# New durations and a price for a change of tile shape in the planner that orders a recurrence's instructions

## The chip, the cores and the metric

One core of one Trainium2 chip. The metric is the device time of one execution in microseconds (us); lower is better. Engines: PE is TensorE, DVE is VectorE, ACT is ScalarE, POOL is GpSimd, SP issues most of the DMAs.

## What is computed

One layer of a diffusion backbone over 1024 latent tokens with a prefix of 256 context tokens, width 1024:

```
h = modulate(rmsnorm(x))
u, rw, gates = split(h @ w_in)
a = s5_branch(u)                     # bidirectional complex SSM, then GELU and GLU (two dense products)
b = rwkv7_branch(rw)                 # 16 heads of 64, two directions, the recurrence below, then w_out
x = x + gate * ((sigmoid(ga) * a + sigmoid(gb) * b) @ w_out)
x = x + gate * conv_ffn(modulate(rmsnorm(x)))
out = rmsnorm(x)

# the recurrence, for each head and direction, over 256 + 1024 tokens
S = S * diag(w_t) + (S a_t) b_t^T + v_t k_t^T
y_t = S r_t
```

The token recurrence is computed in chunks of 64 tokens (20 chunks: 4 of context, 16 of latents). Within a chunk it becomes small matrix products, the inverse of a triangular 64x64 matrix for each head, direction and chunk, and a state that passes from chunk to chunk.

## The kernel before, in words

Three stages follow one another. Stage A computes the input projection, the S5 branch and the operands of the recurrence, and stores them to DRAM. Stage B (`stage_b`, line 1519 on) runs the recurrence, and as filler two large dense products. Stage C computes the output projections and the feed-forward part. The change touches stage B alone.

Stage B loops over 8 pairs of heads (`pair`); a pair holds both directions. Its work is written as nodes of a graph (`Node`, line 721), each with an engine, a cost in us, its dependencies and a function that emits its instructions:

- `prep_nodes` (line 905): for a block of 4 chunks and one direction. It loads kk, k and r (line 936), forms the gate projection `zn` on PE (L947, two 64-row products side by side), takes tanh of it twice (L955), a scan (L961), two exponentials (L962, L964), several products on DVE (L966 to L979) and one on POOL (L970), then the score products `sc` (L994, L997) and transposes `tp` (L1022, L1025) on PE in 64x64 tiles, which ACT and DVE copy out (L1002 copies the triangular matrix L).
- `inverse_nodes` (line 1041): for a batch of 8, 8 or 4 chunks (`BATCHES`). It sends L through DRAM into lanes (L1065, L1067), solves 16x16 blocks with 15 products (L1073) and 15 reductions (L1076) on DVE that follow one another, returns the result through DRAM (L1080 to L1088), and joins the blocks by five groups of products in 32x32 tiles (`merge`, L1109, L1115, L1120, L1137, L1142), whose last copies write TX (L1149). One set of lanes and one set of merge tiles serve all batches.
- `chain_nodes` (line 1157): for each chunk the state step. `gx` on PE, X copied by ACT (L1227), `gu` on PE with TX, U copied by DVE (L1244), `gs` on PE, the new state by DVE (L1267); `y` on PE and its copy on ACT (L1287). All its products are in 64x64 tiles (L1184, L1189).
- `final_nodes` (line 1313): for each pair four pieces of 256 tokens. They load y, the bonus, v and the gate from DRAM (L1326), normalise (products at L1330 and L176, small DVE steps at L155 to L163) and store.
- `filler_nodes` (line 1421): two dense products, 512 nodes of three full 128x128 matmuls with 512 columns (L1464, L1465, L1466). One node follows the other; their weights are split into two parts by ACT and DVE (L1443, L1444).

A ring of 5 blocks (`NBLK`) holds the prepared operands. One pair has 5 blocks, so a block's preparation for the next pair begins when the chain has read the same block of this pair and stored its output.

`Plan.order` (line 748) decides the order. It computes a due time for each node, back from the chain's steps through the costs and a lag per engine (`LAG`), stretched by 2. Then it simulates the engines: whichever node is ready and has the earliest due time goes next on its engine, and the engine's clock advances by the node's cost. The list in which nodes were taken is the order in which their instructions are emitted, and PE, ACT and DVE run their instructions strictly in that order (`manual_schedule`, line 1616). On PE the planner keeps a sum of columns (`n.cols`) over the last 3.4 us of its own time:

```python
if total < FORCE or cold and ticks.get(tick, 0.0) < HOT:
    best = pick(fills)
best = best or pick(h)
if best is None and (total < WARM or not left):
    best = pick(fills)
```

So a filler (or a product of a final) goes ahead of the recurrence when the sum is under `FORCE` (3600), and into an empty place when it is under `WARM` (4500). `pick(h)` takes the node with the earliest due time whose PSUM bank is free. The costs are numbers in the code; they are not read from a run, and the planner's time is not the chip's.

Of the kernel before, what the change touches and what calls it, by code (L numbers as in the profile page):

```python
# [720 lines left out]
class Node:  # L721

    __slots__ = ("eng", "cost", "deps", "succ", "emit", "due", "take", "give", "left", "ready", "bank", "cols", "fill", "tag", "key", "pri", "second")

    def __init__(self, eng, cost, deps, emit):
        self.eng, self.cost, self.emit = eng, cost, emit
        self.deps = [x for x in deps if x is not None]
        self.succ, self.due, self.take, self.give, self.ready = [], 1e9, None, None, 0.0
        self.cols, self.fill, self.tag, self.key, self.second = 0.0, None, None, False, None
# [7 lines left out]
class Plan:  # L737
# [19 lines left out]
    def order(self):  # L757
# [43 lines left out]
        def pick(h):  # L801

            skip, best = [], None
# [14 lines left out]
        while True:  # L818
# [8 lines left out]
            for e in heaps:  # L827
# [9 lines left out]
                if h or (e == "p" and fills):  # L837
# [6 lines left out]
                    else:  # L844
# [4 lines left out]
                        best = best or pick(h)  # L849
# [12 lines left out]
            n = best  # L862
            if n.eng == "p":
                hot.append((now, n.cols))
# [8 lines left out]
            end = now + n.cost  # L873
# [30 lines left out]
def prep_nodes(E, g, c0, d, k):  # L904
# [37 lines left out]
    zn.cols = 2048  # L942
# [7 lines left out]
    for half in range(2):  # L950
# [6 lines left out]
        th.append(op("a", 0.36, [zn, ms], tanh, give=zs[half]))  # L957
    ts_ = op("v", 0.2, [th[0]], lambda: nc.vector.tensor_scalar(P[:, :, 1:65], P[:, :, 1:65], 0.5, 0.5, op0=OP.mult,
                                                                op1=OP.add))
    flat = P.rearrange("p c t -> p (c t)")  # L960
    scan = op("v", 0.34, [ts_], lambda: nc.vector.tensor_tensor_scan(flat, E.m65, flat, 0.0, op0=OP.mult, op1=OP.add))  # L961
    epi = op("a", 0.4, [scan], lambda: nc.scalar.activation(PI, P[:, :, 1:65], AF.Exp, scale=KAP,  # L962
                                                             bias=E.ln_half))
    ep = op("a", 0.31, [epi], lambda: nc.scalar.activation(P, P, AF.Exp, scale=-KAP))  # L964
    pc = op("g", 0.1, [ep], lambda: nc.gpsimd.tensor_copy(g.PC.tile[:, d, c0:c0 + nb], P[:, :, 64]))
    q = [op("v", 0.4, [ep, lkk], lambda: nc.vector.scalar_tensor_tensor(  # L966
        Q[:, :, 0:64], v3(o_(kk)), -1.0, P[:, :, 0:64], op0=OP.mult, op1=OP.mult))]
    t1 = op("v", 0.34, [th[1]] + q, lambda: nc.vector.scalar_tensor_tensor(kk, o_(ta), 1.0, kk, op0=OP.add,
                                                                           op1=OP.mult))
    tid = op("g", 0.54, [t1], lambda: nc.gpsimd.tensor_scalar(ta, ta, E.par("ka", j), E.ka2[:, j:j + 1], op0=OP.mult,  # L970
                                                              op1=OP.add))
    tk = op("v", 0.34, [tid, lkx], lambda: nc.vector.tensor_mul(ta, ta, o_(kx)))
    bk = [op("v", 0.4, [t1, epi], lambda: nc.vector.tensor_mul(BK[:, :, 0:64], v3(o_(kk)), PI))]
# [936 lines left out]
```

## Time and profile before

| | us |
|---|---|
| median of 3 runs | 3253.95 |
| lowest, highest run | 3245.26, 3255.84 |
| the profiled execution | 3263.26 |
| its span, first to last instruction | 3261.5 |
| busy in the span: PE, DVE, ACT, POOL | 2911.9, 1838.5, 1371.0, 471.7 |

The rows below come from the one profiled execution. Times in them are us from the start of its span. A row of instruction groups gives the line of the kernel, the engine and operation, output and inputs, the count, then busy us and the mean ns of one, then the idle time of the engine just before them with what ended it. The ends of matmuls are modelled, so the spacing of their starts is the safer reading. "PEld" is the weight load of a matmul. "Clock" is the granted clock of PE as a share of 2.4 GHz: 1.0 is 2.4 GHz, 0.5 is 1.2 GHz. Some matmul records are missing from the trace. A product in float32 has two matmul records.

### The profile page before, as it was taken

How to read it: one execution, taken by the hardware profiler on the slowest of the kernel's cores; microseconds unless marked ns; L12 is line 12 of the kernel's file. 1: busy time of each engine (PE TensorE's matmuls, PEld its weight loads, DVE VectorE, ACT ScalarE, POOL GpSimd, SP SyncE). 2: the span in 40 equal slices, each digit the busy share in tenths (PEclk: the TensorE clock that was granted, in tenths of full speed). 3: DMA queues.
4: the chain of work that ended last, by engine and by line, in shares of the span. 5: the costliest groups of instructions: out<-in, count | busy, mean ns of one | idle time of the engine just before them, and what ended most of it. 6: DMA issues, size and time to landing. Idle time of an engine off the chain costs nothing.

```text
span 3261.5 us, 83856 instructions
## 1 busy us (share of the span) xinstructions
PE 2911.9 (89%) x34806; PEld 2197.0 (67%) x34806; DVE 1838.5 (56%) x4640; ACT 1371.0 (42%) x3055; POOL 471.7 (14%) x781
## 2 busy tenths in 40 slices
PE   6999887878579898999889888899998999999998
PEld 1788676767446666666666666666775888887876
DVE  7668777663345454668575667655534444344343
ACT  5224544435235454555444555442314433333332
POOL 0430011011222222223131222211000000000000
PEclk8999898989789888889788998889998999999999
DMA  5663333333465565455555455544531111113332
GB/s 190 207 168 104 128 117 125 110 119 120 145 167 148 152 161 135 120 135 133 130 143 126 119 141 146 125 125 139 193 120 55 52 48 49 46 52 112 107 107 74
DMA packets 556879, 399.32 MB, mean 122 GB/s; under 512 B 374225, under 2 KB 460497, under 8 KB 555217
## 3 DMA queue, kind: packets, MB, share of 16 engines
q1 hardware_dynamic: 517824, 300.96, 33.5%
q0 software_dynamic: 29312, 87.75, 8.0%
q10 hardware_dynamic: 9360, 5.25, 0.8%
q8 instruction: 273, 4.47, 0.6%
q14 instruction: 110, 0.89, 0.1%
HBM read 286.16 MB, written 112.85 MB: 122 GB/s over the span
## 4 chain that ended last, share of the span: by engine, by line
PE 61%; DMA 11%; issue 9%; DVE 9%; ACT 5%; SPq 3%; POOL 1%; ACTq 0%; DVEq 0%; POOLq 0%
PE pd L202 8%; PE pd L203 8%; PE pd L204 8%; PE bank L1464 5%; PE bank L1465 3%; PE bank L1466 3%; PE bank L1189 3%; PE bank L1184 3%; PE o L1751 3%; PE o L1752 3%; PE o L1753 2%; DMA wraw<-win 2%; PE bank L1330 1%; PE bank L994 1%; PE bank L947 1%
## 5 line engine op out<-in xcount | busy, mean ns | idle before, releaser
L189 DVE TENSOR_TENSOR wlo<-wraw,whi 128x512 fp32r<-128x512 f32 x276 | 184.0, 689 | 493.6 <-ACT whi L188 492.9
L188 ACT ACTIVATE whi<-wraw 128x512 fp32r<-128x512 f32 x276 | 165.8, 627 | 490.8 <-PE pd L203 243.4
L202 PE MATMUL pd<-hh,whi 128*128 128x512 f32 (+1 forms) x744 | 285.8, 384 | 51.8 <-ACT xs L624 35.2
L1464 PE MATMUL bank<-fxh,fwh 128*128 128x512 f32 x512 | 277.4, 542 | 12.1 <-ACT fo L1487 8.6
L202 PE MATMUL pd<-h2h,whi 128*128 128x512 f32 x704 | 275.5, 392 | 12.3 <-ACT h2h L1639 12.2
L204 PE MATMUL pd<-hh,wlo 128*128 128x512 f32 (+1 forms) x744 | 280.9, 378 | 1.5 <-DVE wlo L189 1.5
L203 PE MATMUL pd<-hl,whi 128*128 128x512 f32 (+1 forms) x744 | 282.1, 379 | 0.0
L204 PE MATMUL pd<-h2h,wlo 128*128 128x512 f32 x704 | 278.9, 397 | 0.0
L203 PE MATMUL pd<-h2l,whi 128*128 128x512 f32 x704 | 278.3, 396 | 0.3 <-DVE h2l L1640 0.2
L1465 PE MATMUL bank<-fxl,fwh 128*128 128x512 f32 x512 | 221.2, 432 | 0.5 <-issue 0.5
L1466 PE MATMUL bank<-fxh,fwl 128*128 128x512 f32 x512 | 220.8, 431 | 0.0
L202 PEld LDWEIGHTS pd<-hh,whi 128*128 128x128 f32 x744 | 148.3, 199 | 81.6 <-ACT xs L624 38.3
L204 PEld LDWEIGHTS pd<-hh,wlo 128*128 128x128 f32 x744 | 147.7, 199 | 25.8 <-DVE wlo L189 2.0
L203 PEld LDWEIGHTS pd<-hl,whi 128*128 128x128 f32 x744 | 148.4, 199 | 23.8 <-issue 2.5
L202 PEld LDWEIGHTS pd<-h2h,whi 128*128 128x128 f32 x704 | 133.2, 189 | 45.7 <-ACT h2h L1639 15.6
L203 PEld LDWEIGHTS pd<-h2l,whi 128*128 128x128 f32 x704 | 133.2, 189 | 33.0 <-DVE h2l L1640 2.1
L204 PEld LDWEIGHTS pd<-h2h,wlo 128*128 128x128 f32 x704 | 133.6, 190 | 26.6
L1464 PEld LDWEIGHTS bank<-fxh,fwh 128*128 128x128 f32 x512 | 104.3, 204 | 62.0 <-issue 20.0
L1444 DVE SCALAR_TENSOR_TENSOR fwl<-fr,fwh 128x512 fp32r<-128x512 f32 x128 | 92.6, 724 | 86.9 <-ACT fwh L1443 86.3
L1073 DVE TENSOR_TENSOR PR<-TN,LN 128x1 f32<-128x1 f32 (+9 forms) x360 | 118.5, 329 | 39.8 <-DMA LN<-LD 35.6
L1751 PE MATMUL o<-ph,whi 128*128 128x512 f32 x352 | 137.8, 396 | 2.2 <-ACT p L1725 2.2
L1752 PE MATMUL o<-pl,whi 128*128 128x512 f32 x352 | 138.9, 395 | 0.0
(395 smaller groups left out, 7209.3 us busy)
## 6 DMA issues: line engine op xcount, KB each, us to landing
wraw<-up SPq DMA_DIRECT2D x88, 256.0 KB
wraw<-down SPq DMA_DIRECT2D x88, 256.0 KB
wraw<-win SPq DMA_DIRECT2D x68, 256.0 KB
fin<-wmod SPq DMA_DIRECT2D x32, 512.0 KB
fr<-win SPq DMA_DIRECT2D x64, 256.0 KB
fr<-glu SPq DMA_DIRECT2D x64, 256.0 KB
s5U<-u_d SPq DMA_DIRECT2D x32, 320.0 KB
kk<-kk_d SPq DMA_DIRECT2D x80, 128.0 KB
```

The source lines that it names most:

```text
L188: nc.scalar.activation(hi[:, c], raw, AF.Copy)
L189: nc.vector.tensor_sub(lo[:, c], raw, hi[:, c])
L202: nc.tensor.matmul(pt[:, :n], hi[:, c], xh, start=k == 0, stop=False)
L203: nc.tensor.matmul(pt[:, :n], hi[:, c], xl, start=False, stop=False)
L204: nc.tensor.matmul(pt[:, :n], lo[:, c], xh, start=False, stop=k == 7)
L1073: last = [op("v", 0.07 + k * k / 960.0, last, lambda lo=lo, hi=hi, k=k, s=s: nc.vector.tensor_tensor(out=PR[al, :k * k].rearrange("l (c m) ...
L1184: nc.tensor.matmul(out[OWN[e], d], w[OWN[e]], x[OWN[e]], skip_group_check=True, tile_position=(64 * e, 64 * e), **kw)
L1464: nc.tensor.matmul(o, hi[:, c], xh[:, k, :], start=k == 0, stop=False)
L1465: nc.tensor.matmul(o, hi[:, c], xl[:, k, :], start=False, stop=False)
L1466: nc.tensor.matmul(o, lo[:, c], xh[:, k, :], start=False, stop=k == 7)
L1751: nc.tensor.matmul(o, hi[:, c], ph, start=k == 0, stop=False)
L1752: nc.tensor.matmul(o, hi[:, c], pl, start=False, stop=False)
```

## The change

The instructions stay the same. Three things change in the planner:

1. Each PE node gets a `mode`, the shape of tile that it uses: 128 (the default: fillers, most products of the finals), 96 (`zn`), 64 (scores, transposes, chain), 32 (merge), 48 (`bc`). When the node taken differs in mode from the one before it, `SWITCH` (0.1 us) is added to PE's simulated clock. Among the nodes of the recurrence `pick(h, last)` takes the one with the smallest due time after 0.5 us (`AFFINE`) has been added to those of another mode. Fillers and finals are still taken by `pick(fills)`, without a mode.
2. Costs of nodes become other numbers. PE: `gx`, `gu`, `gs` 0.35 to 0.23, `y` 0.6 to 0.44, `sc` 0.5 and 0.4 to 0.44 and 0.23, `tp` 0.35 to 0.44, merge nodes up by 0.08 to 0.12 in three of the five groups. DVE, ACT and POOL: nearly all up (the diff has them). The filler stays at 0.65; its constant has a name now. Lags, `FORCE`, `WARM`, `PERIOD` and the DMA nodes of SP stay.
3. Two counts of columns: `zn` 2048 to 1024, `tp` 0 to 1024.

```diff
-        def pick(h):
-
+        last = 128
+
+        def pick(h, mode=None):
+
+
+            if mode is not None:
+                ok = [x for x in h if x[2].take is None or len(self.free[x[2].take]) > (x[2].second is not None)]
+                if not ok:
+                    return None
+                x = min(ok, key=lambda x: (x[0] + AFFINE * (x[2].mode != mode), x[1]))
+                h.remove(x)
+                heapq.heapify(h)
+                return x[2]
...
-                        best = best or pick(h)
+                        best = best or pick(h, last)
...
             n = best
+            shape = 0.0
             if n.eng == "p":
+                shape, last = SWITCH * (n.mode != last), n.mode
...
-            end = now + n.cost
+            end = now + n.cost + shape
...
     zn = op("p", 0.44, gates, None, take="F")
-    zn.cols = 2048
+    zn.cols, zn.mode = 1024, 96
...
-        th.append(op("a", 0.36, [zn, ms], tanh, give=zs[half]))
+        th.append(op("a", 0.47, [zn, ms], tanh, give=zs[half]))
...
-    scan = op("v", 0.34, [ts_], lambda: nc.vector.tensor_tensor_scan(flat, E.m65, flat, 0.0, op0=OP.mult, op1=OP.add))
+    scan = op("v", 0.69, [ts_], lambda: nc.vector.tensor_tensor_scan(flat, E.m65, flat, 0.0, op0=OP.mult, op1=OP.add))
...
-    tid = op("g", 0.54, [t1], lambda: nc.gpsimd.tensor_scalar(ta, ta, E.par("ka", j), E.ka2[:, j:j + 1], op0=OP.mult,
+    tid = op("g", 0.96, [t1], lambda: nc.gpsimd.tensor_scalar(ta, ta, E.par("ka", j), E.ka2[:, j:j + 1], op0=OP.mult,
...
-        w = op("p", (0.5 if lat else 0.4), sc[-1:] or bk + [bkk] + q + rq, None, take=None if h else "F")
+        w = op("p", (0.44 if lat else 0.23), sc[-1:] or bk + [bkk] + q + rq, None, take=None if h else "F")
...
-    tp.emit = tr
+    tp.emit, tp.cols, tp.mode = tr, 1024, 64
...
-        last = [op("v", 0.07 + k * k / 960.0, last, lambda lo=lo, hi=hi, k=k, s=s: nc.vector.tensor_tensor(
+        last = [op("v", 0.14 + k * k / 520.0, last, lambda lo=lo, hi=hi, k=k, s=s: nc.vector.tensor_tensor(
...
-        last = [op("v", 0.07 + k * k / 960.0, last, lambda lo=lo, hi=hi, k=k, s=s: nc.vector.tensor_reduce(
+        last = [op("v", 0.14 + k * k / 960.0, last, lambda lo=lo, hi=hi, k=k, s=s: nc.vector.tensor_reduce(
...
-        gx = op("p", 0.35, state + B.q[0] + B.q[1] + kt + first, None)
+        gx = op("p", 0.23, state + B.q[0] + B.q[1] + kt + first, None)
...
-            sp = [op("a", 0.24, state + [B.pc[d], w], lambda d=d: nc.scalar.activation(
+            sp = [op("a", 0.34, state + [B.pc[d], w], lambda d=d: nc.scalar.activation(
...
-            y = op("p", 0.6, [eu] + B.y[0] + B.y[1], None)
+            y = op("p", 0.44, [eu] + B.y[0] + B.y[1], None)
...
-                    g.done.append(op("g", 1.0, B.out, lambda d=d: nc.gpsimd.dma_start(
+                    g.done.append(op("g", 0.55, B.out, lambda d=d: nc.gpsimd.dma_start(
...
-            r = op("v", 0.07, [r] if i else [r, pv], f, **({} if i else {"give": pv}))
+            r = op("v", 0.2, [r] if i else [r, pv], f, **({} if i else {"give": pv}))
...
+FILL = 0.65
+SWITCH, AFFINE = 0.1, 0.5
...
-            n = add("a", 0.48, [last, g], lambda: nc.scalar.activation(dst, src(), AF.Tanh, scale=0.5), give=first)
+            n = add("a", 0.78, [last, g], lambda: nc.scalar.activation(dst, src(), AF.Tanh, scale=0.5), give=first)
```

## Rows read from the trace of the kernel before

**Rows 1.** The page: busy tenths of PE and its granted clock in 40 slices.

```profile
PE   6999887878579898999889888899998999999998
PEclk8999898989789888889788998889998999999999
```

**Rows 2.** Busy time by stretch of stage B; PEclk is the mean granted clock.

```profile
core 0: us, PE busy (x) PEld busy (x) DVE busy (x) ACT busy (x) POOL busy (x), PEclk, DMA share, GB/s
917.00:978.00 61.00, 55.17 (x885) 34.02 (x886) 35.93 (x104) 28.56 (x65) 16.51 (x24) 0.91 0.66 164
978.00:2228.00 1250.00, 1124.61 (x24650) 796.29 (x24648) 769.13 (x2509) 612.73 (x1753) 296.92 (x475) 0.87 0.54 136
2228.00:2281.00 53.00, 49.24 (x276) 37.01 (x275) 31.58 (x123) 11.79 (x25) 5.41 (x10) 1.00 0.42 136
```

**Rows 3.** ACT in order of time, 1590 to 1715 us, lines L1002, L1149 and L1227.

```profile
1590.41 0.39 ACT L1002 ACTIVATE L<-bank 128x256 f32<-128x256 f32 x1 [0.41 <-DVE RB L1008]
...
1634.52 0.38 ACT L1002 ACTIVATE L<-bank 128x256 f32<-128x256 f32 x1 [2.25 <-PE bank L994]
...
1676.16 0.28 ACT L1227 ACTIVATE X<-bank 128x128 f32<-128x128 f32 x1 [1.08 <-PE bank L1184]
...
1709.30 0.78 ACT L1149 ACTIVATE TX<-bank 32x256 f32<-32x256 f32 x2 [0.33 <-PE bank L1142]
...
1714.01 0.28 ACT L1227 ACTIVATE X<-bank 128x128 f32<-128x128 f32 x1 [0.40 <-PE bank L1184]
```

**Rows 4.** Groups of PE instructions between 917 and 2232 us.

```profile
L1464 PE MATMUL bank<-fxh,fwh 128*128 128x512 f32 x469 | 258.2, 551 | 9.6 <-ACT fo L1487 8.6 <-DVE fo L1504 0.4 <-ACT fwh L1443 0.3
L997 PE MATMUL bank<-Q,BK 64*64 64x128 f32 (+1 forms) x1216 | 95.8, 286 | 8.0 <-DVE BK L974 3.4 <-DVE fin L1351 1.2 <-issue 1.2
L1184 PE MATMUL bank<-X,TX 64*64 64x64 f32 x1280 | 75.5, 239 | 4.7 <-ACT X L1227 4.3 <-ACT TX L1149 0.4
L1189 PE MATMUL bank<-V,BT 64*64 64x64 f32 x1216 | 72.7, 240 | 11.3 <-DVE S L1267 10.0 <-DVE TN L1076 0.5
L1184 PE MATMUL bank<-U,BT 64*64 64x64 f32 x1216 | 71.4, 239 | 19.8 <-DVE U L1244 19.3
L1109 PE MATMUL bank<-AT,L 16*16 16x16 f32 x2560 | 31.3, 177 | 23.6 <-DMA AT<-AD 15.6 <-DVE RB L1008 5.3 <-issue 2.5
L1330 PE MATMUL bank<-fin,center 128*128 128x256 f32 x54 | 23.2, 519 | 22.6 <-DVE fin L1336 19.1 <-DVE TN L1076 2.5 <-ACT BT L1028 1.0
```

**Rows 5.** Groups of DVE instructions between 917 and 2232 us.

```profile
L1073 DVE TENSOR_TENSOR PR<-TN,LN 128x1 f32<-128x1 f32 (+9 forms) x360 | 118.5, 329 | 39.8 <-DMA LN<-LD 35.6
L1076 DVE TENSOR_REDUCE TN<-PR 128x1 f32<-128x1 f32 (+9 forms) x360 | 83.4, 232 | 4.7
L961 DVE TENSOR_TENSOR_SCAN P<-m,P 128x260 f32<-128x260 f32 x76 | 52.8, 694 | 1.0
```

**Rows 6.** PE in order of time at the full clock, 1408 to 1410 us.

```profile
1408.51 0.23 PE L1184 MATMUL bank<-U,BT 64*64 64x64 f32 x2
1408.67 0.50 PE L1464 MATMUL bank<-fxh,fwh 128*128 128x512 f32 x1
1409.00 0.40 PE L1465 MATMUL bank<-fxl,fwh 128*128 128x512 f32 x1
1409.23 0.40 PE L1466 MATMUL bank<-fxh,fwl 128*128 128x512 f32 x1
1409.56 0.45 PE L1184 MATMUL bank<-RB,U 64*64 64x64 f32 x8
```

**Rows 7.** All engines in order of time, 1608 to 1615 us: a final's load and what follows.

```profile
1608.37 0.37 SPq L1326 DMA_DIRECT2D fin<-y_d  x1
...
1612.12 0.43 DVE L1336 TENSOR_TENSOR fin<-fin 128x256 f32<-128x256 f32 x1 [6.12 <-DMA fin<-y_d]
...
1612.60 1.22 PE L1330 MATMUL bank<-fin,center 128*128 128x256 f32 x2 [3.38 <-DVE fin L1336]
...
1613.25 0.99 PE L1464 MATMUL bank<-fxh,fwh 128*128 128x512 f32 x1
...
1615.03 1.06 PE L1137 MATMUL bank<-AT,L 32*32 32x32 f32 x32
```

**Rows 8.** Groups of PE instructions between 2228 and 2285 us.

```profile
L1464 PE MATMUL bank<-fxh,fwh 128*128 128x512 f32 x45 | 20.2, 450 | 2.6 <-ACT fo L1497 1.4 <-DVE fo L1504 1.2
```

**Rows 9.** PE in order of time, 2276 to 2277 us: two fillers in a row.

```profile
2276.17 0.39 PE L1464 MATMUL bank<-fxh,fwh 128*128 128x512 f32 x1
...
2276.85 0.39 PE L1464 MATMUL bank<-fxh,fwh 128*128 128x512 f32 x1
```

More of the change, by code (lines that the diff above doesn't have):

```diff
@@ L721 @@
 class Node:
-    __slots__ = ("eng", "cost", "deps", "succ", "emit", "due", "take", "give", "left", "ready", "bank", "cols", "fill", "tag", "key", "pri", "second")
+    __slots__ = ("eng", "cost", "deps", "succ", "emit", "due", "take", "give", "left", "ready", "bank", "cols", "fill", "tag", "key", "pri", "second", "mode")
     def __init__(self, eng, cost, deps, emit):
@@ L728, in __init__ @@
         self.succ, self.due, self.take, self.give, self.ready = [], 1e9, None, None, 0.0
-        self.cols, self.fill, self.tag, self.key, self.second = 0.0, None, None, False, None
+        self.cols, self.fill, self.tag, self.key, self.second, self.mode = 0.0, None, None, False, None, 128
 LAG = {"p": 0.27, "a": 0.22, "v": 0.22, "g": 0.25, "s": 2.2, None: 0.0}
@@ L998, in mm @@
                                      stop=True, tile_position=(64 * e, 64 - 64 * e))
-        w.emit, w.cols = mm, 8 * nn
+        w.emit, w.cols, w.mode = mm, 8 * nn, 64
     first = sc[0]
@@ L1011, in prep_nodes @@
             give=sb)
-    mq = [op("g", 1.2 if lat else 0.7, [cp], lambda: nc.gpsimd.tensor_mul(
+    mq = [op("g", 1.33 if lat else 0.74, [cp], lambda: nc.gpsimd.tensor_mul(
         A[:, :, 0:nn], A[:, :, 0:nn], E.mask[:, None, 0:nn].to_broadcast([128, 4, nn])))]
-    tp = op("p", 0.35, bk + [bkk, blk.gate], None, take="F")
+    tp = op("p", 0.44, bk + [bkk, blk.gate], None, take="F")
     tb = pl.second(tp)
@@ L1101, in go @@
                     mm(pz, i, c00 + i)
-            w.emit = go
+            w.emit, w.mode = go, 32
         return ws[0], ws[-1], lambda: E.ps(ws[0])[:, 0:n * width].rearrange("p (c t) -> p c t", t=width)
@@ L1121, in mm3 @@
                              tile_position=(s, s))
-    cost16 = 0.06 + m / 75.0
+    cost16 = 0.16 + m / 75.0
     f, w, pz = merge(at, 0.105, 16, mm1)
@@ L1225, in g1 @@
                     own(pX, d, Q[:, d, s, 0:64], S.tile[:, d], start=False, stop=True)
-        gx.emit, gx.cols = g1, 512
-        ex = op("a", 0.3, [gx, X.renew()], lambda: nc.scalar.activation(X.tile, pX, AF.Copy))
+        gx.emit, gx.cols, gx.mode = g1, 512, 64
+        ex = op("a", 0.28, [gx, X.renew()], lambda: nc.scalar.activation(X.tile, pX, AF.Copy))
         sp = []
@@ L1240, in g2 @@
                 own(pU, d, tx[:, d, si, :], X.tile[:, d], start=end and d == 0, stop=True)
-        gu.emit, gu.cols = g2, 512
+        gu.emit, gu.cols, gu.mode = g2, 512, 64
         X.users.append(gu)
@@ L1256, in g3 @@
                     own(pS, d, BT[:, d, s, 0, :], U.tile[:, d], start=False, stop=True)
-            gs.emit, gs.cols = g3, 512
+            gs.emit, gs.cols, gs.mode = g3, 512, 64
             U.users.append(gs)
@@ L1267, in update @@
                     nc.vector.scalar_tensor_tensor(SN.tile[:, d], pS[:, d], pc, SP.tile[:, d], op0=OP.mult, op1=OP.add)
-            state = [op("v", 0.25, [gs, w, B.pc[d]] + sp, lambda d=d: update(d)) for d in HALF]
+            state = [op("v", 0.28, [gs, w, B.pc[d]] + sp, lambda d=d: update(d)) for d in HALF]
             for x in state:
@@ L1458, in dense @@
                 k = 4 * half + q
-                n = add("p", 0.65, x[k] + parts, None, take=None if first else "D")
+                n = add("p", FILL, x[k] + parts, None, take=None if first else "D")
                 first = first or n
@@ L1496, in evac_b @@
             sb, g = outs.next()
-            n = add("a", 0.48, [last, g], lambda: nc.scalar.activation(sb.tile, E.ps(first), AF.Tanh), give=first)
+            n = add("a", 0.6, [last, g], lambda: nc.scalar.activation(sb.tile, E.ps(first), AF.Tanh), give=first)
             hold[0] = sb, n
```

77 lines of the change are left out of this document (39 added, 38 removed).

## The prediction

> **What bounds the kernel now.** I read the slices of the span first: PE is busy nearly throughout, and in the middle its clock falls below full speed in many slices [rows 1]. Then the stretches of stage B. Between the chain's first state step (978 us) and its last (2228 us) PE is busy for 1125 of 1250 us, DVE for 769 and ACT for 613, and PE's mean granted clock is 0.87 [rows 2]. With the two levels 2.4 and 1.2 GHz that mean is 2 x 0.13 x 1250 = 325 us at the lower level. What follows the last step takes 53 us at the full clock [rows 2]. The change can act between 917 and 2281 us only.
>
> Then the pace of the chain. A pair takes about 1250 / 8 = 156 us, and in the pair shown it is set by a loop of latencies, not by one engine: the L of the batch of chunks 8 to 15 is copied out between 1590.4 and 1634.9 us, its TX is ready at 1710.1, and the chain, whose preceding step copied X at 1676.2, copies the next at 1714.0 [rows 3]. It stood still for 38 us there. Meanwhile PE worked on fillers and other pairs' products. So two things hold the time: how late each link of that loop comes in the strict queues, and how much work PE does in all. Fillers fill the difference, and 45 of them were left when the chain had ended [rows 8].
>
> Then what PE waits for. Of its idle time a good part ends with a DVE or ACT instruction: U 19.3 us, S and TN 10.5, the evacuation of fillers 9.3, X and TX 4.7, RB 5.3, products before the scores 4.6, others 3.5, in all 57 us; 15.6 us end with AT from DRAM and 19.1 with a final's first sum [rows 4], which itself stands behind a load (6.1 us of DVE in the case shown) [rows 7].
>
> **The change, part by part.**
>
> *The durations.* The old plan believes DVE much faster than it is. The products of the inverse are 0.07 + k²/960, on average 0.156 us over k = 1 to 15, against 0.329 measured; the reductions 0.156 against 0.232; the scan 0.34 against 0.694 [rows 5]. Over 360, 360 and 76 instructions that is 62 + 27 + 27 = 116 us of DVE work that the plan doesn't know. The new costs average 0.299, 0.226 and 0.69. On PE the filler counts 0.65, but its start to the next node's start is 0.89 us at the full clock [rows 6]; the new plan reaches 0.65 plus two changes, 0.85, in such a place. The chain's nodes fall by 0.12, which a change gives back. So the new plan is slower in its own time and nearer to the chip's, and an instruction is less often queued in front of another that was ready. I give this 30% of the 57 us of PE's waits on DVE and ACT: **-17 us**. Bounds: 0 and -57; nearer to 0, since the order stays a forecast and each engine's lateness hangs on the others'.
>
> *The price of a shape.* A filler's last start is followed by the next product of its own kind after 0.23 us, and by a 64x64 product after 0.33; the way back is 0.16 between starts where 64x64 products keep some 0.06 [rows 6]. So a change costs about 0.10 us, as the planner now says. Most changes stay: 469 fillers [rows 4] are put in by the column sum, and the affinity doesn't see them, so up to 938 changes are out of its reach. In reach are `zn` and merge nodes: 76 `zn` (one for each scan [rows 5]) and 35 merge nodes for a pair, 280 in all, two changes each: 712 at most, -71 us; none at the other end. An affinity of half a microsecond against due times stretched by 2 moves few nodes; I take a tenth: **-7 us**.
> By the Trainium skill (TensorEngine Tiling (Array Packing), Key Properties) a change of tiling mode drains the array, and a change of tile within a mode does not. Its page TensorE: Matmul & The Clock Gate (Step-by-step) puts the drain at about 128 cycles, 0.053 us at 2.4 GHz as an estimate; by that the term would be -4 us. The 0.10 of the rows is what the sum uses.
>
> *The clock.* Where the queue makes PE wait, the granted clock falls afterwards. The stretch from 1612.6 us on runs at the lower level after PE stood 3.4 us behind a final's load: there a filler took 1613.25 to 1615.03, 1.78 us, not 0.89 [rows 6, 7]. Fewer such waits leave less time at the lower level. The new counts of columns only move 1024 from `zn` to `tp`, 0 in the sum over a preparation. If a tenth of the 325 us goes to full speed, half of it is saved: **-16 us**. Bounds: half of it gone, -81; half as much again, +81. I stay near zero because the waits on DRAM, which keep their lags and SP costs, stand behind many of these stretches.
>
> *The fillers' pace.* Fillers are drawn by the plan's time. Along the loop the plan becomes longer: 30 DVE steps of the inverse +5.3 us by the numbers above, one preparation about +1.6 (scan +0.35, POOL product +0.42, tanh, exponentials and products +0.8), copies and merge nodes about +2, in all about 9 us for each pair, some 6% of 156. At a constant column rate (a pair draws about 78,000 columns of its own and (512 - 45) / 8 = 58 fillers of 1536) 6% are about 6 fillers for each pair, 48 in all: just the 45 that are now left over. These take 0.68 us each at the end [rows 9], 31 us; the finals of the last pair and their loads remain there, so I take -20 of the 31. In the loop they cost 45 x 0.89 = 40 us of PE, against 125 us in which PE is idle there [rows 2]; I charge 15. Together **-5 us**, between -31 and +40.
>
> *Loads of the finals.* The y stores on POOL are now planned 0.45 us shorter, and the loads behind them keep their lag, so consumers may be queued earlier against a DMA that isn't faster. 32 finals x 0.45 = 14 us at most, none at least: **+4 us**. SP's queue carries no new instruction, and its order follows the plan.
>
> *Everything else* is emitted as before: stage A up to 917 us and stage C from 2281 us on, 0.
>
> Sum: -17 - 7 - 16 - 5 + 4 = -41 us. The profiled execution took 3263.3 us, which gives 3222; it lay 9.3 us above the median of the runs, so against the median I forecast **3213 us**. A difference of about 0.3% (10 us) is what a measurement of this kernel can tell from none.
>
> **The rivals.**
>
> *The same time.* The loop is made of things that no cost changes: four trips through DRAM for each batch, one set of lanes, five blocks. The 38 us of standing still [rows 3] would then be there again, and PE's queue would look nearly as before. It speaks for it that DMA waits (34.7 us [rows 4]) are untouched; against it, that L alone took 44 us to come out. Time 3254, within 3244 to 3264. To this belongs that the change doesn't do what it says: if the affinity hardly ever decides, term two is 0, and only 7 us of the forecast go.
>
> *Slower.* The place is PE's queue between 978 and 2228 us. The longer plan draws 45 more fillers into the loop, and they don't land in idle places but ahead of merge, scores and chain. They cost 0.89 us at the full clock and up to 1.78 at the lower one [rows 6, 7], so 40 to 80 us, and 31 come back at the end: +9 to +49, I take +25: 3254 + 25 = 3279. It decides if PE's busy time before the last step grows by more than its idle time shrinks. For it: the merge products wait in PE's strict queue behind whatever was planned before them, and a forced filler goes ahead of ready work. Against it: PE idles 125 us there, and nothing in the new plan asks for more columns per unit of its time.
>
> *Much faster.* If the in-order waits halve and a third of the 325 us goes to full speed, terms one and three become -28 and -54, the sum -90: 3164. For it: DVE's 116 unknown us lie in the loop itself. It is the low end of the first case.
>
> **How the numbers follow.** Faster, in all shades below 3244: 0.53, of which 0.06 below 3150. The same: 0.14. Slower: 0.33, of which 0.10 above 3295, where the clock would lose as well (half of its bound, +40, on top of +9). So the range 3150 to 3295 leaves out 0.16. The likeliest case alone has 3165 to 3244. Chances: faster 0.53, same 0.14, slower 0.33.
>
> **What would show it.** In the changed kernel's stretches the last state step should come near 2190 us if the forecast holds; the mean clock between first and last step should rise from 0.87 to about 0.88 or 0.89; the waits of PE on U and S should fall below 25 us together; fillers left after the last step should be well under 45. The inverse's rows must keep their durations, or the comparison is off. I'm wrong if the chain's period stays at 156 us with fewer fillers left (then the plan's length drew them and nothing else changed), if the clock falls below 0.85, or if the waits on loads of finals grow by more than 15 us.

## The result, and the profile after

The changed kernel took 3272.3 us in the median of 20 runs (3262.0 to 3283.5), the kernel before, run beside it, 3250.5 us (3230.7 to 3267.9): a ratio of 1.0076 [1.0057, 1.0094] (the two medians alone give 1.0067). The forecast was 3213 us, faster; it came out slower by 0.8%. Medians and ratios here and below leave out executions more than 1.5% longer than the kernel's fastest, which matters most for `before_more`: four of its 12 are left out, and its loop and tail come from one of them, of 3277.0 us.

Here the same stretches of the changed kernel as in [rows 2]: up to the chain's first state step, the loop (first to last state step), and from there to the first product of stage C, which I call the tail. The last column but two is the mean granted clock.

```profile
core 0: us, PE busy (x) PEld busy (x) DVE busy (x) ACT busy (x) POOL busy (x), PEclk, DMA share, GB/s
917.00:984.00 67.00, 64.12 (x944) 39.56 (x938) 39.52 (x115) 31.27 (x71) 19.14 (x28) 0.83 0.71 178
984.00:2239.00 1255.00, 1121.25 (x24702) 796.26 (x24698) 761.77 (x2509) 617.87 (x1758) 301.35 (x472) 0.88 0.54 136
2239.00:2298.00 59.00, 33.93 (x167) 22.66 (x165) 26.82 (x120) 7.53 (x17) 5.39 (x10) 0.65 0.35 113
```

[rows 2] end with PE's last filler, at 2281 us; stage C's first product came at 2287 us, so the tail of the kernel before is 59 us and not 53:

```profile
2228.00:2287.00 59.00, 49.24 (x276) 37.01 (x275) 34.10 (x130) 14.30 (x28) 5.95 (x11) 0.97 0.46 150
```

The loop takes 1255 us where [rows 2] show 1250, and the tail 59 us as before, but PE is busy in it for 34 us and not 49, and its clock is 0.65, where it had been 0.97. The profiled execution before was among its longer ones: 3263.3 us, 12.7 above the median of its runs in this comparison, while the one after, 3270.7, is near its median. A nearly identical order, `before_lag` below, left a profile of a usual execution, and it is the better one to compare with:

```profile
984.00:2199.00 1215.00, 1088.04 (x24550) 771.58 (x24550) 756.92 (x2472) 609.07 (x1740) 286.86 (x465) 0.90 0.54 138
2199.00:2271.00 72.00, 52.69 (x280) 39.37 (x273) 38.90 (x147) 15.01 (x30) 6.47 (x12) 0.87 0.41 135
```

So the changed plan's loop is 40 us longer and its tail 13 us shorter. Of the 40 us PE is busy for 33 more and idle for 7 more (133.8 against 127.0). The groups of PE between 917 and 2243 us of the changed kernel (lines have moved by 13, those of the fillers by 16):

```profile
L1480 PE MATMUL bank<-fxh,fwh 128*128 128x512 f32 x508 | 270.1, 532 | 9.5 <-ACT fo L1503 6.9 <-DVE fo L1520 1.2 <-ACT fo L1513 1.0
...
L1197 PE MATMUL bank<-X,TX 64*64 64x64 f32 x1280 | 74.1, 236 | 11.1 <-ACT X L1240 10.2 <-issue 0.8
L1202 PE MATMUL bank<-V,BT 64*64 64x64 f32 x1216 | 71.3, 237 | 19.4 <-DVE S L1280 12.8 <-DVE U L1257 6.0
L1197 PE MATMUL bank<-U,BT 64*64 64x64 f32 x1216 | 70.6, 237 | 14.5 <-DVE U L1257 14.5
...
L1122 PE MATMUL bank<-AT,L 16*16 16x16 f32 x2560 | 30.8, 178 | 17.5 <-DMA AT<-AD 12.7 <-issue 3.2 <-ACT P L968 1.2
...
L1343 PE MATMUL bank<-fin,center 128*128 128x256 f32 x52 | 22.6, 523 | 25.1 <-DVE fin L1349 23.5 <-ACT P L977 0.6 <-ACT BT L1041 0.4
```

The same waits in the loop of `before_lag`:

```profile
L1184 PE MATMUL bank<-X,TX 64*64 64x64 f32 x1272 | 74.9, 239 | 3.9 <-ACT X L1227 3.7
L1189 PE MATMUL bank<-V,BT 64*64 64x64 f32 x1208 | 70.9, 236 | 24.4 <-DVE S L1267 14.7 <-DVE TN L1076 6.9 <-DVE S L1265 1.6
L1184 PE MATMUL bank<-U,BT 64*64 64x64 f32 x1216 | 69.9, 236 | 19.3 <-DVE U L1244 15.2 <-DVE TN L1076 3.8
```

The waits on U and S moved little: 12.8 + 6.0 + 14.5 = 33.3 us, against 29.3 in [rows 4] and 31.5 in `before_lag`. That on X grew from 4.3 (3.7) to 10.2, and that on a final's first sum from 19.1 to 23.5. Two groups of DVE over the same stretch, the inverse's products and the finals' first sum, and the latter in the kernel before:

```profile
L1086 DVE TENSOR_TENSOR PR<-TN,LN 128x1 f32<-128x1 f32 (+9 forms) x360 | 112.3, 312 | 49.8 <-DMA LN<-LD 46.9
...
L1349 DVE TENSOR_TENSOR fin<-fin 128x256 f32<-128x256 f32 x26 | 12.2, 467 | 51.7 <-DMA fin<-y_d 51.5
```

```profile
L1336 DVE TENSOR_TENSOR fin<-fin 128x256 f32<-128x256 f32 x27 | 15.2, 562 | 38.5 <-DMA fin<-y_d 38.5
```

DVE stands 46.9 us for L from DRAM (35.6 in [rows 5]). After the last step only eight fillers are left, against 45 in [rows 8]; PE's group after 2239 us:

```profile
L1480 PE MATMUL bank<-fxh,fwh 128*128 128x512 f32 x8 | 3.3, 416 | 0.0
```

And yet the tail is as long as before. What fills it is seen in order of time, 2274 to 2292 us, in the lines that belong to one final: POOL's store of the final before, SP's load, DVE's sum, PE's product, the next store, and the first load of stage C:

```profile
2274.61 0.54 POOL L1370 DMA_DIRECT2D yg_d<-fin  x1 [4.36 <-DVE fin L1368]
...
2277.48 0.32 SPq L1339 DMA_DIRECT2D fin<-y_d  x1
...
2279.91 0.43 DVE L1349 TENSOR_TENSOR fin<-fin 128x256 f32<-128x256 f32 x1 [5.59 <-DMA fin<-y_d]
...
2280.39 1.22 PE L1343 MATMUL bank<-fin,center 128*128 128x256 f32 x2 [6.59 <-DVE fin L1349]
...
2288.99 0.54 POOL L1370 DMA_DIRECT2D yg_d<-fin  x1 [13.83 <-DVE z L1737]
...
2291.27 0.80 SPq L1679 DMA_DIRECT2D ygt<-yg_d  x2
```

The finals of the first seven pairs share one slot of SBUF (`NFIN` is 1; the last pair's four may also take three blocks that have come free). So a final's load waits until the one before has been stored: one after another, 14.4 us from store to store here. Stage C waits for the last of them. My prediction took this row of finals as a fixed remainder.

### The profile page after: what moved, and what is told of

The parts are those of the page before. It is cut to its first block, busy times and chain, and to the rows that moved or that the text cites. A ratio compares the mean times of both kernels' runs of the same rounds, so it can differ in the third digit from the quotient of the medians.

```text
span 3268.9 us, 83829 instructions
## 1 busy us (share of the span) xinstructions
PE 2902.3 (89%) x34806; PEld 2187.1 (67%) x34806; DVE 1829.2 (56%) x4640; ACT 1372.5 (42%) x3055; POOL 478.1 (15%) x781
## 4 chain that ended last, share of the span: by engine, by line
PE 61%; DMA 12%; issue 10%; DVE 7%; ACT 6%; SPq 3%; POOL 1%; ACTq 0%; DVEq 0%; POOLq 0%
PE pd L202 8%; PE pd L203 8%; PE pd L204 7%; PE bank L1480 5%; PE bank L1481 3%; PE bank L1482 3%; DMA wraw<-win 3%; PE bank L1202 3%; PE bank L1197 3%; PE o L1767 3%; PE o L1768 2%; PE o L1769 2%; PE bank L1343 2%; PE bank L1007 2%; PE bank L960 1%
## 5 line engine op out<-in xcount | busy, mean ns | idle before, releaser
L202 PEld LDWEIGHTS pd<-h2h,whi 128*128 128x128 f32 x704 | 133.0, 189 | 44.5 <-ACT h2h L1655 13.7
L1086 DVE TENSOR_TENSOR PR<-TN,LN 128x1 f32<-128x1 f32 (+9 forms) x360 | 112.3, 312 | 49.8 <-DMA LN<-LD 46.9
L1769 PE MATMUL o<-ph,wlo 128*128 128x512 f32 x352 | 136.5, 392 | 0.0
```

Of the source, the lines that this page charges most:

```text
L202: nc.tensor.matmul(pt[:, :n], hi[:, c], xh, start=k == 0, stop=False)
L1086: last = [op("v", 0.14 + k * k / 520.0, last, lambda lo=lo, hi=hi, k=k, s=s: nc.vector.tensor_tensor(out=PR[al, :k * k].rearrange("l (c m) ...
L1769: nc.tensor.matmul(o, lo[:, c], ph, start=False, stop=k == 21)
```

## The experiments

All runs in one table. "In" are fillers between the first and last state step, "left" those after; "finals" are stored after the last step (four are the last pair's own, always). Loop and tail in us, from one profiled execution each; the ratio is the time against the kernel before, run beside it, with its 95% interval.

| run | fillers in / left | finals | loop | tail | ratio |
|---|---|---|---|---|---|
| before | 434 / 45 | 6 | 1250 | 59 | 1 |
| changed | 466 / 8 | 7 | 1256 | 59 | 1.0076 [1.0057, 1.0094] |
| no_switch | 424 / 48 | 14 | 1197 | 165 | 1.0241 [1.0209, 1.0274] |
| pe_only | 433 / 43 | 6 | 1255 | 54 | 1.0038 [1.0013, 1.0063] |
| others_only | 472 / 0 | 10 | 1222 | 102 | 1.0118 [1.0086, 1.0150] |
| warm4000 | 440 / 33 | 9 | 1234 | 93 | 1.0163 [1.0129, 1.0197] |
| ns_finals | 445 / 27 | 4 | 1273 | 42 | 1.0071 [1.0046, 1.0095] |
| before_finals | 436 / 42 | 4 | 1258 | 49 | 1.0052 [1.0029, 1.0074] |
| before_lag | 436 / 43 | 7 | 1215 | 72 | 0.9988 [0.9961, 1.0014] |
| no_affine | 473 / 1 | 8 | 1247 | 74 | 1.0107 [1.0080, 1.0135] |
| before_more | 477 / 0 | 7 | 1237 | 75 | 1.0028 [0.9994, 1.0062] |
| before_fewer | 390 / 94 | 7 | 1190 | 100 | 0.9999 [0.9970, 1.0028] |
| after_fewer | 392 / 86 | 6 | 1238 | 93 | 1.0130 [1.0092, 1.0169] |
| after_both | 407 / 69 | 5 | 1243 | 74 | 1.0093 [1.0056, 1.0129] |
| before_slots | 429 / 51 | 4 | 1197 | 55 | 0.9917 [0.9878, 0.9956] |
| others_slots | 447 / 27 | 4 | 1221 | 41 | 0.9922 [0.9895, 0.9949] |
| pe_slots | 440 / 36 | 4 | 1212 | 42 | 0.9958 [0.9928, 0.9989] |
| after_slots | 433 / 41 | 4 | 1223 | 48 | 0.9979 [0.9949, 1.0009] |
| ns_slots | 387 / 91 | 4 | 1200 | 88 | 1.0025 [0.9991, 1.0060] |
| cols_slots | 440 / 32 | 4 | 1246 | 42 | 1.0078 [1.0047, 1.0109] |

### Which part of the change

The first theory was that the price of a change of shape makes the plan longer and so draws the fillers in. In the changed kernel, without price and affinity:

```diff
-SWITCH, AFFINE = 0.1, 0.5
+SWITCH, AFFINE = 0.0, 0.0
```

> The changed kernel with SWITCH and AFFINE at 0: all new durations and column counts, no price of a shape. Its plan leaves 48 fillers after the chain's last step, where the changed kernel leaves 8 and the kernel before 45. Theory pace (the loss comes from fillers drawn into the loop): about the time of before, 3245 to 3258. Theory order (the new durations make an order that is worse in itself, whatever the fillers): about the changed kernel's, 3265 to 3280. Theory hit (the forecast was right about the durations, and only the price of a shape did harm): below before by 10 or more, 3240 or less.

3313.7 us, far worse, and outside all three ranges. The loop did become short and 48 fillers stayed, as the theory has it, but the tail is 165 us. The timeline of POOL in it shows why, three stores of finals in a row:

```profile
2258.95 0.54 POOL L1370 DMA_DIRECT2D yg_d<-fin  x1 [13.21 <-DVE fin L1368]
...
2272.91 0.54 POOL L1370 DMA_DIRECT2D yg_d<-fin  x1 [13.42 <-DVE fin L1368]
...
2286.59 0.54 POOL L1370 DMA_DIRECT2D yg_d<-fin  x1 [13.13 <-DVE fin L1368]
```

and the windows show the loop, the tail, and 40 us within it:

```profile
974.00:2171.00 1197.00, 1071.11 (x24407) 771.22 (x24405) 723.80 (x2357) 602.78 (x1726) 292.11 (x457) 0.88 0.53 133
2171.00:2337.00 166.00, 90.58 (x419) 63.70 (x416) 67.23 (x262) 20.22 (x44) 10.83 (x20) 0.67 0.31 103
2240.00:2280.00 40.00, 14.98 (x50) 9.04 (x50) 12.74 (x52) 2.25 (x6) 1.63 (x3) 0.50 0.22 73
```

14 finals come after the last step, and where they run alone they take 13.7 us each, with PE busy for 15 of 40 us at the lower clock. From this run on, the row of finals is the second theory.

The changed kernel with the old costs of ACT, DVE and POOL, that is PE's part alone, and the kernel before with the new costs of ACT, DVE and POOL alone; one line of each:

```diff
-    scan = op("v", 0.69, [ts_], ...
+    scan = op("v", 0.34, [ts_], ...
```

> The PE half alone: new PE costs, modes, SWITCH, AFFINE and column counts; ACT, DVE and POOL keep the old costs. 43 fillers are left after the last step. Theory pace: about before, 3245 to 3260. Theory order: a loss of its own, some half of the 22 us, 3258 to 3270. If the price of a shape does the harm by itself, whatever the pace: 3265 or more.

```diff
-    scan = op("v", 0.34, [ts_], ...
+    scan = op("v", 0.69, [ts_], ...
```

> The other half alone: new costs of ACT, DVE and POOL, PE as before and no price of a shape. No filler is left after the last step. Theory pace: like the changed kernel or worse, 3270 to 3285, with the last step later than 2235 us and a tail of some 45 us that holds no fillers. Theory hit (truer durations bring the queues closer): 3240 or less, whatever the pace.

PE's part alone 3251.6 us, +0.4%; the other durations alone 3277.0 us, +1.2%. Both times are what the pace theory asked for, but the second by another way: the last step came early (2203 us, not after 2235), and 10 finals with a tail of 102 us at clock 0.53 lost it again:

```profile
981.00:2203.00 1222.00, 1102.93 (x24616) 786.16 (x24608) 739.58 (x2448) 615.53 (x1746) 295.69 (x465) 0.90 0.54 137
2203.00:2304.00 101.00, 47.63 (x196) 30.33 (x190) 39.08 (x174) 9.23 (x22) 6.50 (x12) 0.53 0.28 93
```

So the halves don't add. By the plan's counts the price stretches PE's planned time, and more finals go into the loop with it: of the 14 of `no_switch` 7 remain in the changed kernel.

The changed kernel with fewer fillers in empty places, and without the affinity:

```diff
-FORCE, WARM = 3600.0, 4500.0
+FORCE, WARM = 3600.0, 4000.0
```

> The changed kernel with WARM 4000 for 4500: everything of the change stays, fewer fillers go into empty places, 33 are left after the last step. Theory pace: back by two thirds of the loss, 3252 to 3262. Theory order: no change, 3265 to 3280. If the empty places were what kept the clock up, slower than the changed kernel, 3280 or more.

```diff
-SWITCH, AFFINE = 0.1, 0.5
+SWITCH, AFFINE = 0.1, 0.0
```

> The changed kernel with AFFINE 0: the price of a shape alone, without the preference for the same shape. 1 filler and 8 finals are left after the last step, where the changed kernel has 8 and 7. Theory finals: one more final behind the last step, 3270 to 3290, the changed kernel's time or up to 14 us more. If the preference is worth its changes of shape (12 of 1193): within 3 us of the changed kernel.

3287.1 and 3280.9 us. The first is slower than the changed kernel, as the last line of its expectation has it, but not through the clock of the loop (0.89): it has two more finals and 34 us more of tail. Without the affinity there are 1207 changes of shape between first and last step, counted in the order of the matmuls by the planner's modes, with it 1195, before the change 1198. So the affinity moves about 12 of 1200, and the run's one more final (+15 us of tail) can carry its loss against the changed kernel.

### The finals pulled forward

```diff
-FDUE, GDUE = 8.0, 0.0
+FDUE, GDUE = 8.0, -300.0
```

in `no_switch` and in the kernel before. `GDUE` is the due time that the finals get.

> SWITCH and AFFINE 0, all new durations, and GDUE -300 for 0: on ACT, DVE and among the fillers the finals' nodes go ahead of others, so that 4 finals are left after the chain's last step, where the version without it has 14 and before 6; 27 fillers are left. Theory finals (the time lost is the row of finals that run one after another, 13.7 us each, behind the last step): the last step comes near 2200 us, 2171 plus what ten finals add on PE, DVE and ACT, the first product of stage C some 55 us after it, and the time is 3215 to 3240, 70 us or more below the version without it and at or below before. Theory order (the new durations' order is poor in itself): 3300 or more.

> The kernel before with GDUE -300: old durations, 4 finals and 42 fillers left after the last step, where before has 6 and 45. Theory finals: little is to be had, since 4 of the 6 belong to the last pair anyway; 3225 to 3245, that is 0 to 15 us below before. If putting finals ahead holds up the recurrence instead: 3250 or more.

3265.5 us, 48 less than `no_switch` (2.41% above the kernel before there, 0.71% here), though short of what was expected, and 3261.4 us, 17 more than before, in the range of "holds up the recurrence". Ten finals fewer in the tail take 123 us from it (165 to 42), 12.3 each; the loop grows by 76 us (1197 to 1273), with ten finals and 21 fillers more in it. That finals which are due early go ahead of the recurrence follows from the code; that they hold it up fits both loops (`before_finals` has 1258 us at the fillers of `before_lag`, which has 1215), but no wait was followed to show it.

### Any new order, and the fillers alone

A small new lag in the kernel before gives an order that is nearly the old one:

```diff
-LX, LS = 0.02, 1.5
+LX, LS = 0.021, 1.5
```

> The kernel before with LX 0.021 for 0.02, a lag longer by a nanosecond, which means nothing on the chip but gives another order: 43 fillers and 7 finals left. It measures how far an order that is neither better nor worse by design may fall from before. Theory finals: one more final behind the last step, 0 to 14 us slower. Theory order (any new order loses against one that happens to be good): 10 us or more slower.

3242.6 us, 0.9988: not every new order loses. It is one order, though; how far orders of equal worth scatter can't be told from one. Then the fillers of the kernel before, more and fewer, and fewer in the changed kernel, in one also with finals pulled forward:

```diff
-FORCE, WARM = 3600.0, 4500.0
+FORCE, WARM = 4000.0, 5000.0
```

> The kernel before with FORCE 4000 and WARM 5000 for 3600 and 4500: old durations and no price of a shape, but as many fillers between the chain's first and last step as the changed kernel has (477 by the plan, 466 there, 433 to 436 before) and the changed kernel's 7 finals behind it. Theory pace (each filler in the loop adds 1.0 to 1.4 us, and the tail is set by the finals that are left): 3265 to 3295, the changed kernel's loss without its durations. Theory durations (the order from the new durations is what loses): 3235 to 3255.

```diff
-FORCE, WARM = 3600.0, 4500.0
+FORCE, WARM = 3000.0, 4100.0
```

> The kernel before with FORCE 3000 and WARM 4100: 390 fillers in the loop, 94 left behind the last step with 7 finals. Theory pace: 46 fillers fewer in the loop are 46 to 64 us, and the tail of some 70 us has room for 94 fillers at 0.68 us, so 3185 to 3215. Theory clock (fillers keep the clock up, and without them the loop is as long): 3240 or more, with more time at the lower clock between first and last step than 320 us.

```diff
-FORCE, WARM = 3600.0, 4500.0
+FORCE, WARM = 3000.0, 3400.0
```

> The changed kernel with FORCE 3000 and WARM 3400: all of the change, 392 fillers in the loop, 86 left and 6 finals behind the last step. Theory pace: as the kernel before at the same pace, 3185 to 3225. Theory durations: 20 us or more above the kernel before at the same pace. If the new durations do bring the queues closer to the chip, as was forecast: 15 us or more below it.

```diff
-FORCE, WARM = 3600.0, 4500.0
+FORCE, WARM = 3000.0, 3800.0
...
-FDUE, GDUE = 8.0, 0.0
+FDUE, GDUE = 8.0, -300.0
```

> The changed kernel with FORCE 3000, WARM 3800 and GDUE -300: 407 fillers in the loop, 69 left and 5 finals behind the last step. Theory pace: 15 fillers more in the loop than at FORCE 3000 and WARM 3400, +15 to +20, and one final less in the tail, -12: 3190 to 3230. If finals that go ahead hold up the recurrence, as the two runs with GDUE -300 suggest: 3235 or more.

3255.0, 3243.6, 3284.1 and 3270.4 us. The pace theory missed all four. `before_more`, with more fillers in its loop than the changed kernel and as many finals behind it, is at 1.0028, not clear of none, where the changed kernel is at 1.0076. `after_both` is slow as the finals pulled forward had it (3235 or more). The windows of `before_fewer`, and the tail of `before_more`:

```profile
982.00:2172.00 1190.00, 1061.28 (x24427) 756.61 (x24420) 747.20 (x2463) 597.81 (x1726) 288.63 (x462) 0.88 0.54 137
2172.00:2273.00 101.00, 87.01 (x444) 66.61 (x443) 51.20 (x167) 24.73 (x47) 8.63 (x16) 0.99 0.46 153
```

```profile
2229.00:2304.00 75.00, 36.17 (x154) 23.08 (x154) 30.22 (x133) 7.91 (x18) 4.85 (x9) 0.55 0.28 94
```

Against `before_lag`, with as many finals, 46 fillers fewer shorten the loop by 25 us: 0.54 us for a filler in the loop. That is two single profiles, and `before_fewer` has 36 us more at the lower clock (288 against 253); with half of these taken out, the price would be 0.92 us. But 94 fillers then fill a tail of 100 us at the full clock, and nothing is won. Seven finals with no filler beside them make a tail of 75 us (`before_more`), with 43 fillers one of 72 (`before_lag`): the finals set it. By the two prices the 30 fillers that the changed kernel has more in its loop than `before_lag` cost 16 to 28 of its 40 us. They aren't all of the loss: `after_fewer` has as few fillers as `before_fewer` and one final fewer in its tail, and its loop is still 48 us longer, the whole 1.3% slower than the kernel before. This is against the pace of the fillers as the only cause.

### A second slot for the finals

If the row of finals is the cost, two slots take it away, and what remains of the change shows. To make room in SBUF, one of the three buffers of filler weights is given up; no run has that alone:

```diff
-NBLK, NRAW, NW, NOUT, NFIN = 5, 3, 3, 3, 1
+NBLK, NRAW, NW, NOUT, NFIN = 5, 3, 2, 3, 2
```

in `no_switch`, in the changed kernel, in the kernel before, and in the two halves of the change:

> SWITCH and AFFINE 0 with all new durations, and NFIN 2 and NW 2 for 1 and 3: a second slot for the finals, paid with a pair of filler weights. 4 finals are left behind the chain's last step (14 without the second slot), and 91 fillers. Theory finals (the loss without a price of a shape is the row of finals in one slot): 3205 to 3245, some 70 to 100 us below the same kernel with one slot. Theory order (the new durations lose for another reason): 3270 or more.

> The changed kernel with NFIN 2 and NW 2. 4 finals and 41 fillers left (7 and 8 with one slot). Theory finals and pace together: 3235 to 3262, 10 to 35 us below the changed kernel. Theory order: 3265 or more.

> The kernel before with NFIN 2 and NW 2: 4 finals and 51 fillers left (6 and 45 with one slot). Theory finals: up to 25 us below before, 3218 to 3243. If the second slot or the missing pair of weights costs something by itself (loads that come earlier and collide, fillers that wait for weights): above 3250, and then the other three carry that too.

> The new costs of ACT, DVE and POOL alone with NFIN 2 and NW 2: 4 finals and 27 fillers left (10 and none with one slot). Theory finals: 3235 to 3260, 17 to 40 us below the same with one slot. Theory order: 25 us or more above the kernel before with two slots.

> The PE half of the change (new PE costs, price of a shape, modes, column counts; old costs of ACT, DVE and POOL) with the second slot: 4 finals and 36 fillers left. It closes the square of before_slots (3213), others_slots (3215) and after_slots (3235). Theory PE half (what is left of the loss once the row is gone comes from the PE costs and the price): 3228 to 3245. Theory pace alone: 15 fillers more in the loop than before_slots at about half a microsecond, 3215 to 3227. Theory interplay (neither half loses, only both together): 3208 to 3218.

In all of them just the last pair's four finals come after the last step. `no_switch` fell to 3254.1 us, 1.0025 for 1.0241, which is neither theory's range (its 91 fillers now make the tail, 88 us at clock 0.99); the changed kernel to 3235.2, at the edge of what was expected. The kernel before fell to 3213.3 and the other durations alone to 3214.9, both further than expected; PE's part alone to 3224.3, in the range of the pace alone. The sums of DVE that begin the four finals of the tail in `before_slots` follow one another at 3 to 5 us:

```profile
2186.98 0.42 DVE L1336 TENSOR_TENSOR Q<-Q 128x256 f32<-128x256 f32 x1
...
2191.59 0.42 DVE L1336 TENSOR_TENSOR Q<-Q 128x256 f32<-128x256 f32 x1
...
2195.31 0.42 DVE L1336 TENSOR_TENSOR Q<-Q 128x256 f32<-128x256 f32 x1
...
2198.49 0.42 DVE L1336 TENSOR_TENSOR fin<-fin 128x256 f32<-128x256 f32 x1
```

With the slot, the new durations of ACT, DVE and POOL cost nothing (0.9922 [0.9895, 0.9949] against 0.9917 [0.9878, 0.9956]), where they had cost 1.2% without; their tail fell from 102 us to 41 and their loop stayed (1222, 1221), so that loss was the row of finals. They gain nothing either. The slot shortens the other loops too: the changed kernel's from 1256 to 1223 us, that of the kernel before to 1197, from 1215 in `before_lag`; so not all that it gives is at the end of the stage. The whole change still costs 0.6% (3235.2 against 3213.3; the intervals of the two ratios just meet), with about the same number of fillers in the loop. PE's part alone comes out 0.4% above, which the intervals don't tell from none. The windows of `before_slots`, then of `after_slots`:

```profile
981.00:2179.00 1198.00, 1086.35 (x24590) 775.13 (x24589) 752.43 (x2543) 612.47 (x1755) 298.25 (x476) 0.90 0.54 139
2179.00:2233.00 54.00, 47.51 (x244) 36.15 (x241) 28.55 (x98) 13.96 (x26) 5.40 (x10) 1.00 0.42 144
```

```profile
984.00:2207.00 1223.00, 1101.97 (x24596) 794.02 (x24588) 767.19 (x2540) 609.05 (x1753) 301.18 (x476) 0.87 0.53 135
2207.00:2255.00 48.00, 40.45 (x211) 30.93 (x211) 25.73 (x94) 13.05 (x24) 4.85 (x9) 0.99 0.40 135
```

Here it is the loop, 25 us longer: PE is busy in it for 16 us more, at a clock of 0.87 for 0.90, and idle for 9 us more. A further suspect in PE's part was the count of columns, since it decides when a filler is drawn. The changed kernel with the slot and the old counts:

```diff
-    zn.cols, zn.mode = 1024, 96
+    zn.cols, zn.mode = 2048, 96
...
-    tp.emit, tp.cols, tp.mode = tr, 1024, 64
+    tp.emit, tp.mode = tr, 64
```

> The changed kernel with the second slot and the old column counts (zn 2048, tp 0): 4 finals and 32 fillers left. If the new counts are what the PE half loses (the plan holds a preparation's columns to come later than they do): 3210 to 3225. If they are not: 3232 to 3245, after_slots and some 9 fillers more in the loop.

3262.0 us, 0.8% above the kernel before beside it and about 1% above `after_slots`, slower than both theories had it: the new counts help. What remains is PE's new costs, or the price. `ns_slots`, without the price, has 42 fillers fewer in its loop than `before_slots` and no shorter loop, which speaks against the price as the sole cause; no run has the price alone.

## Why the prediction was wrong

The step that failed is the one from truer costs to shorter waits: -17 us for PE's waits in order, and on top of it -16 us at the clock, because fewer waits were to leave less time at the lower level. In its place the runs show that PE's waits on U and S grew (33.3 us, against 29.3 and 31.5), that the truer costs of ACT, DVE and POOL bring nothing (0.9922 with them, 0.9917 without, two slots in both), and that the changed loop has 290 us at the lower clock where `before_lag` has 253, by half of the difference an estimated 18 us lost. These two terms make 51 of the some 63 us between the forecast of -41 and the 22 by which the median rose. The terms one by one:

**The fillers' pace.** That the longer plan draws the left-over fillers into the loop was foreseen, and their number came out near (45 forecast, 37 fewer left), though with a slip in the working: 15 products and 15 reductions of the inverse, by the averages given there, add 15 x (0.299 - 0.156) + 15 x (0.226 - 0.156) = 3.2 us and not 5.3. With that the plan grows by 7 us for each pair, and the same reckoning gives some 38. But "-20 of the 31" was to come back in the tail, since I took the finals as a fixed remainder that fits beside whatever is there. The tail is 59 us as before, 13 less than in `before_lag`: it is the row of finals through one slot, at 13.7 us each where it runs alone, and fewer fillers leave that row standing, with PE idle for 25 of 59 us and its clock at 0.65. In the loop +15 was charged, and 30 fillers at 0.54 to 0.92 us give 16 to 28. So the term is about +3 to +15 against `before_lag` instead of -5.

**The durations.** -17 forecast; about 0 measured, by `others_slots` against `before_slots` (3214.9 and 3213.3 us; the intervals leave some 15 us either way, and 18 more fillers in its loop are part of it). The numbers in the plan were indeed far from the rows, and that was my reason. But PE's waits on U and S went to 33.3 us instead of below 25, and X's from 4.3 to 10.2: a truer length didn't bring the links of the loop earlier. Alone and with one slot they even cost 1.2%, since the finals fall behind in the plan; that mishap the prediction didn't have at all.

**The shape.** -7 forecast, from a tenth of 712 changes. The loop has 1195 changes where it had 1198, and the affinity by itself took away 12 (1207 without it). At the 0.10 us of [rows 6] that is 0.3 us for the whole change and 1.2 us for the affinity. By the Trainium skill (TensorEngine Tiling (Array Packing), Key Properties) a change of tiling mode drains the array. No run here tells more of that price than those rows do, as the number of changes stayed.

**The clock.** -16 forecast. The mean in the loop did go from 0.87 to 0.88, but the 0.87 belonged to a long execution. Summed over the loop from the trace's granted clock, 321 us are at the lower level in the profile before, 253 in `before_lag`, 290 in the changed kernel: 37 more than the usual, of which half, 18 us of the 40, is an estimate of what they cost; the other sign. With the fillers' 16 to 28 that makes 34 to 46 against the 40 us; the two overlap, since a filler at the lower level takes longer. The trace also tells what PE did before the clock fell. In the 5 us ahead of a fall it was idle for 2.4 us on average in the changed kernel and for 1.7 us in `before_lag`, where 5 us of either loop hold 0.5 (5 us is a length chosen for this count, nothing of the chip's). So the falls follow gaps in PE's queue, as the forecast had it. But there were 24 of them against 26, and the clock then stayed low for 12.1 us on average instead of 9.7: the number of falls isn't what grew. The same is seen at equal fillers: `after_fewer` 352 us at the lower level, `before_fewer` 288, half of the difference 32 of the 48 us between their loops.

**The loads.** +4 forecast. DVE's wait for y grew from 38.5 us to 51.5, that for L from 35.6 to 46.9; what of these 24 us reaches the end, no run tells. Such a sum says little by itself: `before_slots`, the fastest, waits for L as long as the changed kernel (49.3 us over the same stretch).

**The rivals.** "Slower" gave 3279, +25, by 45 more fillers in PE's queue. The sign, the place and the number of fillers were right, and the difference of the two spans to compare, 3268.9 - 3244.3 = 24.6 us, is the same by luck more than by its terms: a filler costs 0.54 to 0.92 us where 0.89 to 1.78 was charged, 13 us came back and not 31, and with 74 fillers less the changed plan is no faster. "The same" expected the standing still to stay, and of the waits this is true. What made me prefer the gain was the trust that costs nearer to the rows give a better order; it had no row behind it. Of the signs of being wrong that the prediction named, the first came true: the chain's period is 1255 / 8 = 157 us with fewer fillers left. But it wasn't true that nothing else had changed, as `after_fewer` shows.

**What stays open.** Why the whole change still loses 0.6% once the row of finals is gone, and whether PE's part alone (0.9958 [0.9928, 0.9989] against 0.9917 [0.9878, 0.9956]) loses anything. The 0.6% lie in the loop and show as more time at the lower clock, 307 us in `after_slots` and 242 in `before_slots`, with 28 falls in each; what makes the low stretches longer, no run tells. The counts of columns are excluded, and between costs and price no run decides. With one neutral order measured, it may also be no more than one order's luck against another's.

The version that beats both is the kernel before with the second slot (and a buffer of filler weights less), 3213.3 us, 0.83% below the kernel before in the same comparison.

## What to carry to other kernels

In a planned order, ask of a change of costs first what is paced by the plan's time: here fillers and finals are, and both ended up elsewhere. A row of load, compute and store through one slot at the end of a stage sets that end, so count its items and their pitch (13.7 us) before a gain in the work beside it is booked; here a second slot gave 0.8%, and the truer costs nothing. And compare profiles of usual executions: the profile before was 35 us longer in the loop than that of nearly the same order.

## What was not expected of the hardware

- One program's executions scatter by about 0.6% to either side (3230.7 to 3267.9 us over 20). Two profiles of nearly one order, before and `before_lag`, differ by 35 us in the loop. PE is idle there for 125 and 127 us, and has 68 us more at the lower clock in the longer one (321 and 253), half of which is 34: the difference is in how fast PE went and not in how long it waited.
- Where PE has 15 us of work spread over 40 us, in the row of finals of `no_switch`, its granted clock is 0.50, the lower level, throughout; where 94 fillers fill a tail with seven finals (`before_fewer`) it is 0.99. With seven finals, a tail without fillers is as long as one with 43 (75 and 72 us), at a clock of 0.55 and 0.87.
